# A state space mixer whose inputs are turned inside the gated embedding before it, and convolution taps queued behind each head's normalisation

## The chip, the cores and the metric

The kernel runs on one core of one Trainium2 chip. The metric is the device time of one execution in microseconds, as the median of several runs; less is better.

## What is computed

A token block of 512 rows by 1024 features passes two layers and then a second block. Each layer is a mixer, a convolutional feed-forward net and a gated embedding (`ple`), each with a residual. Layer 0's mixer is a gated MLP beside attention; layer 1's mixer is a complex state space model. The second block has two SwiGLU nets around a mixer of eight retention heads and a 31-tap depthwise convolution. The change touches these parts of the reference:

```python
def s5_mixer(u, ...):            # u = rms_norm(x, norm_mix[1])
    ...
    bu_re = jnp.einsum('gpc,bsgc->bsgp', bb_re, uf)
    bu_im = jnp.einsum('gpc,bsgc->bsgp', bb_im, uf)
    ...
    _, _, xr, xi = lax.associative_scan(_complex_affine_combine, (a_r, a_i, bu_re, bu_im), axis=1)
    y = (jnp.einsum('gcp,bsgp->bsgc', c_re.astype(f32), xr)
         - jnp.einsum('gcp,bsgp->bsgc', c_im.astype(f32), xi)
         + d.astype(f32).reshape(S5_GROUPS, S5_GROUP_CH) * uf)
...
        # end of each layer of the first block
        gate = jax.nn.sigmoid(rms_norm(x) @ ple_w_gate[i])
        x = x + gate * (p[i] @ ple_w_proj[i])
...
    # in the second block's mixer
    r = retention_chunkwise(q, k, v)
    r = ((r - mu) * lax.rsqrt(var + LN_EPS)).reshape(bsz, s, V_W) * ret_gn_g.astype(jnp.float32)
    ...
    u = lax.conv_general_dilated(u, conv_k, window_strides=(1,), padding=[(CONV_WIDTH - 1, 0)], ...)
```

## The kernel before

The activations lie in SBUF as eight tiles `x[0..7]` of 128 features by 512 tokens. A float32 product is made from three matmuls: both operands are split into a high and a low part (`Xh`, `Xl`, `whi`, `wlo`) and the low-by-low product is left out (L365 to L367). Weights come in the order of a list: `fetch` loads a raw tile by a DMA of SP's queue, `cook` (L339, L342) lets ACT cast the high part and DVE or POOL (GpSimd) subtract the low part, one tile ahead of the matmuls.

Each engine, and each queue of DMA issues (SP's and ACT's here), works strictly in order. Which order that is follows from the order in which the Python code is written and from a scheduler of the framework, which places instructions of one engine by its own estimates; tiles come from pools with a fixed number of buffers, and a write to a reused buffer waits for its last reader.

**The state space stage** stands between the gated embedding of layer 0 and the gated linear unit behind the mixer. Before it, the statistics of the RMS norm are summed (L204), spread over all partitions by a product of `diag` with ones (L197) and copied to `st_r` (L198). Then each of the eight groups k of 128 channels is a `Unit`:

- `drive` (L1226): DVE multiplies `x[k]` by gain and `st_r` into `h`, whose write to memory (`hd`, L1228) ACT's queue issues;
- `lift` (L1234): SP's queue reads it back in four pieces with time and channels turned, as `up`;
- `load` (L1221): SP's queue loads three tables, `tG`, `tE`, `tC`, two DMAs each;
- `mid`: 16 matmuls with `tG` (L1241, "feed" below), then six DVE operations with `tE` (L1244 to L1249, "spin" below), which rotate real and imaginary parts;
- `scan`: two scans on DVE (L1260), then six products and sums on POOL (L1267 to L1273; for odd k the real part's subtraction, L1269, on DVE), which give `xr` and `xi`;
- `emit`: 24 matmuls with `tC` (L1281), a GELU on ACT (L1283), and a way out through memory again (`y`, L1288);
- `land`: `y` is split into `Gh` and `Gl` for the matmuls of the linear unit ("G matmuls" below).

The loop over t runs `mid` of unit t, `scan` of t−1, `emit` of t−2, `land` of t−3 and the G matmuls of t−4. Of the two weight tiles that are held for the linear unit the first one's matmuls follow in the loop, the second one's after it.

**The heads.** Four rounds h2 of two heads each. `retain` takes the statistics of a head's 512x256 result from PSUM (L1606, L1607), copies the variances into `gnv` (L1610), forms the reciprocal root in `rstd_of` (L174 to L182, with a square root on ACT), and writes the normalised `rn` (L1613); `turn` has PE transpose `rn` (L1620). `taps(n)` issues n taps of the convolution (L1519), each one DVE operation that adds a shifted, scaled tile into PSUM.

Of the kernel before, what the change touches and what calls it, by code (L numbers as in the profile page):

```python
# [18 lines left out]
P = 128  # L19
# [30 lines left out]
def tile_net(ctx: ExitStack, tc: tile.TileContext, a, out):  # L50
# [273 lines left out]
    def cook(i):  # L324
        if i < len(plan):
# [16 lines left out]
            lo.tensor_tensor(lw, rv, hi.bitcast(F32), op=ALU.subtract)  # L342
# [857 lines left out]
    rms2 = Rms()  # L1200
    rb2 = ple(0, X, rms, rms2.add, (rms2.fin1, rms2.fin2))

    with tc.tile_pool(name="s5r", bufs=1) as rp:
# [5 lines left out]
        class Unit:  # L1209
# [4 lines left out]
            def load(self):  # L1214
                k = self.k
                self.G = rp.tile([P, 4, 256], F32, tag="tG", name=nm("tG"), bufs=2)
                self.E = rp.tile([P, 4, 256], F32, tag="tE", name=nm("tE"), bufs=2)
                self.C = rp.tile([P, 4, 448], F32, tag="tC", name=nm("tC"), bufs=2)
                for t, lo, hi in ((self.G, 0, 256), (self.E, 704, 960), (self.C, 256, 704)):
                    for i in range(2):  # L1220
                        nc.sync.dma_start(t[:, 2 * i:2 * i + 2, :],  # L1221
                                          tabs[2 * k + i].rearrange("p (q n) -> p q n", q=2)[:, :, lo:hi])

            def drive(self):
                h = rp.tile([P, 4, P], F32, tag="h", name=nm("h"), bufs=2)
                vec.scalar_tensor_tensor(h, x[self.k].rearrange("p (n j) -> p j n", j=4), col("norm_mix", KD + self.k),  # L1226
                                         rb2.rearrange("p (n j) -> p j n", j=4), op0=ALU.mult, op1=ALU.mult)
                nc.scalar.dma_start(hdr[self.k], h)  # L1228

            def lift(self):  # L1230
                self.up = rp.tile([P, 4, P], F32, tag=f"Gh{self.k}", name=nm("up"))
                src = hdr[self.k].rearrange("(i c) j n -> j c i n", c=32)
# [3 lines left out]
            def mid(self):  # L1236
                k, up = self.k, self.up
                self.pv = pv = [bank((P, 4, P)) for _ in range(2)]
                for z in range(2):
                    for i in range(4):  # L1240
                        pe.matmul(pv[z][:, i, :], self.G[:, i, P * z:P * z + P], up[:, i, :], start=True, stop=True)  # L1241
# [8 lines left out]
                self.rm = xt_(f"X{'hl'[self.par]}5")  # L1250
                act.copy(self.rm, r4[:, 4 * k:4 * k + 4].unsqueeze(2).to_broadcast([P, 4, P]))
                pool.memset(self.rm[:, :, 0:1], 0.0)

            def scan(self):
                k = self.k
                er, ei = self.E[:, :, 0:P], self.E[:, :, P:]
                zr = rp.tile([P, 4, P], F32, tag=f"Gl{k}", name=nm("zr"))
                zi = rp.tile([P, 4, P], F32, tag="zi", name=nm("zi"), bufs=2)
                for z, w in ((zr, self.pv[1]), (zi, self.pv[0])):
                    vec.tensor_tensor_scan(z.rearrange("p i n -> p (i n)"), self.rm.rearrange("p i n -> p (i n)"),  # L1260
                                           w.rearrange("p i n -> p (i n)"), 0.0, op0=ALU.mult, op1=ALU.add)
                self.xr = rp.tile([P, 4, P + 1], F32, tag="xr", name=nm("xr"), bufs=2)
# [3 lines left out]
                t = [xt_(f"X{'hl'[self.par]}{j}") for j in (2, 3)]  # L1266
                pool.tensor_tensor(t[0], er, zr, op=ALU.mult)  # L1267
                pool.tensor_tensor(t[1], ei, zi, op=ALU.mult)
                (vec if k % 2 else pool).tensor_tensor(self.xr[:, :, 1:], t[0], t[1], op=ALU.subtract)  # L1269
                v = [rp.tile([P, 4, P], F32, tag=f"v{j}", name=nm("v")) for j in range(2)]  # L1270
                pool.tensor_tensor(v[0], er, zi, op=ALU.mult)
                pool.tensor_tensor(v[1], ei, zr, op=ALU.mult)
                pool.tensor_tensor(self.xi[:, :, 1:], v[0], v[1], op=ALU.add)  # L1273

            def emit(self):
                k = self.k
                py = bank((P, 4, P))
                for i in range(4):
                    for st, (c, rhs) in enumerate(((320, self.up[:, i, :]), (32, self.xr[:, i, 0:P]),
                                                   (192, self.xi[:, i, 0:P]))):  # L1280
                        pe.matmul(py[:, i, :], self.C[:, i, c:c + P], rhs, start=st == 0, stop=st == 2)  # L1281
                g = rp.tile([P, 4, P], F32, tag="h", name=nm("g"), bufs=2)
# [7 lines left out]
            def land(self):  # L1290
                k = self.k
                G.h[k], G.l[k] = [rp.tile([P, T], F32R, tag=f"G{z}{k}", name=nm(f"G{z}")) for z in "hl"]
# [3 lines left out]
        units[0].load()  # L1296
        for u in units:
            u.drive()
        units[0].lift()
        units[1].load()  # L1300
        for u in units[1:]:
            u.lift()
        acc0, w0s = {}, {}
        for t in range(KD + 4):
            if t and t + 1 < KD:
                units[t + 1].load()
            if t < KD:
                units[t].mid()
            if 0 <= t - 1 < KD:
                units[t - 1].scan()  # L1310
# [4 lines left out]
            if 0 <= t - 3 < KD:  # L1315
                units[t - 3].land()
# [536 lines left out]
```

## Time and profile before

| what | us |
|---|---|
| median of 3 runs (2784.18 to 2787.91) | 2787.21 |
| the profiled execution's own time | 2786.97 |
| its span in the trace | 2785.2 |
| TensorE (PE) busy | 2698.1 |
| DVE busy | 1581.5 |
| ACT busy | 992.5 |
| POOL busy | 666.9 |

All durations below come from this one execution. PE is the engine with the most work; the others matter where PE waits for them. The row of the granted clock (PEclk) says at what share of its full speed PE ran in each of 40 slices.

### The profile page before, as it was taken

Reading aid. Unit: us, or ns where it says so; the run is one execution under the profiler, and the core shown is the slowest. Engines: PE = TensorE matmul, PEld = TensorE weight load, DVE = VectorE, ACT = ScalarE, POOL = GpSimd, SP = SyncE. Lnnn points to the kernel's source line nnn. Section 1 sums busy time; section 2 is a strip of 40 time slices with the busy share of each in tenths; the row PEclk is TensorE's granted clock in tenths of the full one; section 3 lists DMA queues with packets and bytes.
Section 4 is the critical chain, followed back from the end, with each engine's and each line's share of the span. In section 5 each row is a group of like instructions: output and inputs, shape, how many; then the busy total and the mean of one; then the engine's idle time right before and its main releaser. Section 6 shows DMA issues by size and latency. Waiting matters only on the chain. (4 is left out here: it accounts for less than half of the span.)

```text
span 2785.2 us, 35089 instructions
## 1 busy us (share of the span) xinstructions
PE 2698.1 (97%) x14355; PEld 2275.0 (82%) x14355; DVE 1581.5 (57%) x2478; ACT 992.5 (36%) x1295; POOL 666.9 (24%) x590
## 2 busy tenths in 40 slices
PE   8999999999579999999999999999999999999998
PEld 8978888887468888888888888887888788989888
DVE  5456968686654656466333335866387764733335
ACT  5544424344213423244212125333333352432222
POOL 2213035762351000002000026354443421300000
PEclk9999999999789999999999999999999999999999
DMA  5203334433762223224322232322222223222222
GB/s 162 76 31 107 99 105 148 148 132 133 224 207 91 91 91 101 96 76 136 101 96 91 92 105 82 95 82 81 97 81 97 76 91 109 89 91 91 91 95 72
DMA packets 277840, 289.80 MB, mean 104 GB/s; under 512 B 20197, under 2 KB 266951, under 8 KB 277680
## 3 DMA queue, kind: packets, MB, share of 16 engines
q1 hardware_dynamic: 256208, 260.38, 28.8%
q10 hardware_dynamic: 20640, 26.78, 2.7%
q8 instruction: 112, 1.84, 0.3%
q0 software_dynamic: 832, 0.41, 0.1%
q14 instruction: 48, 0.39, 0.0%
HBM read 263.43 MB, written 24.12 MB: 103 GB/s over the span
## 5 line engine op out<-in xcount | busy, mean ns | idle before, releaser
L339 ACT CAST whi<-raw 128x2048 fp32r<-128x2048 f32 (+2 forms) x216 | 406.3, 1881 | 761.4 <-PE ps L366 600.4
L365 PE MATMUL ps<-Xh,whi 128*128 128x512 f32 (+1 forms) x1472 | 567.4, 387 | 0.4 <-ACT Xh L302 0.4
L342 DVE TENSOR_TENSOR wlo<-raw,whi 128x2048 fp32r<-128x2048 f32 (+2 forms) x167 | 381.0, 2282 | 325.9 <-ACT whi L339 324.5
L366 PE MATMUL ps<-Xl,whi 128*128 128x512 f32 (+1 forms) x1472 | 563.0, 383 | 0.6 <-POOL Xl L305 0.6
L367 PE MATMUL ps<-Xh,wlo 128*128 128x512 f32 (+1 forms) x1472 | 562.7, 383 | 0.8 <-DVE wlo L342 0.8
L342 POOL TENSOR_TENSOR wlo<-raw,whi 128x2048 fp32r<-128x2048 f32 (+1 forms) x49 | 223.5, 4561 | 688.1 <-ACT whi L339 362.9
L365 PEld LDWEIGHTS ps<-Xh,whi 128*128 128x128 f32 x1472 | 276.2, 188 | 58.9 <-issue 3.2
L367 PEld LDWEIGHTS ps<-Xh,wlo 128*128 128x128 f32 x1472 | 276.7, 188 | 58.2 <-DVE wlo L342 1.6
L366 PEld LDWEIGHTS ps<-Xl,whi 128*128 128x128 f32 x1472 | 277.1, 188 | 56.9 <-issue 1.2
L365 PE MATMUL ps<-XBh,whi 128*128 128x512 f32 (+1 forms) x736 | 281.9, 385 | 1.0 <-ACT whi L339 1.0
L366 PE MATMUL ps<-XBl,whi 128*128 128x512 f32 (+1 forms) x736 | 281.0, 383 | 0.5 <-POOL XBl L305 0.5
L367 PE MATMUL ps<-XBh,wlo 128*128 128x512 f32 (+1 forms) x736 | 281.4, 384 | 0.0
L366 PE MATMUL ps<-Al,whi 128*128 128x512 f32 (+1 forms) x528 | 202.1, 383 | 1.5 <-DVE Al L305 1.5
L365 PE MATMUL ps<-Ah,whi 128*128 128x512 f32 (+1 forms) x528 | 202.6, 386 | 0.0
L367 PE MATMUL ps<-Ah,wlo 128*128 128x512 f32 (+1 forms) x528 | 202.5, 384 | 0.0
L1519 DVE SCALAR_TENSOR_TENSOR ps<-glu,par,ps 128x512 f32<-128x512 f32 x232 | 174.1, 751 | 4.1
L366 PEld LDWEIGHTS ps<-XBl,whi 128*128 128x128 f32 x736 | 138.2, 188 | 30.3 <-POOL XBl L305 0.9
L367 PEld LDWEIGHTS ps<-XBh,wlo 128*128 128x128 f32 x736 | 138.1, 188 | 29.9
L365 PEld LDWEIGHTS ps<-XBh,whi 128*128 128x128 f32 x736 | 137.6, 188 | 29.3 <-ACT whi L339 1.4
L222 POOL TENSOR_TENSOR st_a<-st_a,st_q 128x512 f32<-128x512 f32 x25 | 44.3, 1770 | 489.4 <-ACT st_q L220 489.3
L374 PE MATMUL ps<-whi,Xh 128*128 128x256 f32 (+1 forms) x512 | 147.6, 289 | 0.7 <-ACT z L608 0.4
L375 PE MATMUL ps<-wlo,Xh 128*128 128x256 f32 (+1 forms) x512 | 144.7, 283 | 0.0
(482 smaller groups left out, 4826.2 us busy)
## 6 DMA issues: line engine op xcount, KB each, us to landing
raw<-in_ffn_w_up_dram SPq DMA_DIRECT2D x66, 1024.0 KB, 5.1
raw<-in_w_in_dram SPq DMA_DIRECT2D x40, 1024.0 KB, 5.1
raw<-in_ffn_w_down_dram SPq DMA_DIRECT2D x32, 1024.0 KB, 4.8
raw<-in_ffn_w_gate_dram SPq DMA_DIRECT2D x22, 1024.0 KB, 5.2
tab<-tabs ACTq DMA_DIRECT2D x16, 960.0 KB, 3.9
raw<-in_ffn_w_down_dram SPq DMA_DIRECT2D x16, 768.0 KB, 4.1
raw<-in_ev_w_in_dram SPq DMA_DIRECT2D x8, 1024.0 KB, 5.2
raw<-in_ple_w_gate_dram SPq DMA_DIRECT2D x8, 1024.0 KB, 4.9
```

Of the source, the lines that this page charges most:

```text
L222: eng.tensor_tensor(self.acc, self.acc, sq, op=ALU.add)
L339: cp = act.copy(hi, rv)
L342: lo.tensor_tensor(lw, rv, hi.bitcast(F32), op=ALU.subtract)
L365: pe.matmul(acc, wh[j][:, s], X.h[k], start=start and t == 0, stop=False)
L366: pe.matmul(acc, wh[j][:, s], X.l[k], start=False, stop=False)
L367: pe.matmul(acc, wl[j][:, s], X.h[k], start=False, stop=stop and t == len(ks) - 1)
L374: pe.matmul(acc, X.h[k][:, s], wh[j], start=start and t == 0, stop=False)
L375: pe.matmul(acc, X.h[k][:, s], wl[j], start=False, stop=False)
L1519: vec.scalar_tensor_tensor(x[m] if t == 30 else acc, u[:, t:t + T], col("ck", t * KD + m), acc, op0=ALU.mult, op1=ALU.add)
```

## The change

Four edits.

1. In `cook`, a low part that POOL computes is subtracted in four quarters, four instructions in place of one.
2. The state space stage. ACT scales each `x[m]` by its gain alone (`turn_in`) as soon as the gated embedding has finished it, and the way through memory to `up` runs while the embedding goes on. After the statistics, `phases` makes one small tile `rbt` from the same product of ones and `diag`, and `norm` multiplies `up` by it: unit 0 on DVE, units 1 to 7 on POOL. Table loads move from SP's to ACT's queue, as separate calls (`load_g`, `load_e`, `load_c`), for units 0 and 1 (but for the latter's `tC`) and `tE` of unit 2 during the embedding; `tE` has three buffers in place of two. `mid` is cut into `feed`, now issued a turn earlier, and `spin`; the real part of an odd unit comes a turn later; unit 7's six products are all on DVE; part of the second weight tile's G matmuls move into the loop.
3. `retain` has no copy to `gnv`; it returns its last instruction.
4. The taps around `retain` are issued after that instruction: 8 (first head) or 24 (second head) taps behind the normalisation, none between statistics and `rn`.

```diff
-            lo.tensor_tensor(lw, rv, hi.bitcast(F32), op=ALU.subtract)
+            q = kt * n // 4 if lo is pool else kt * n
+            for o in range(0, kt * n, q):
+                lo.tensor_tensor(lw[:, o:o + q], rv[:, o:o + q], hi[:, o:o + q].bitcast(F32), op=ALU.subtract)
...
+            def table(self, tag, lo, hi, bufs):
+                t = ep.tile([P, 4, hi - lo], F32, tag=tag, name=nm(tag), bufs=bufs)
+                for i in range(2):
+                    nc.scalar.dma_start(t[:, 2 * i:2 * i + 2, :],
+                                        tabs[2 * self.k + i].rearrange("p (q n) -> p q n", q=2)[:, :, lo:hi])
+                return t
...
+            def turn_in(self):
                 k = self.k
+                h = ep.tile([P, 4, P], F32, tag="h", name=nm("h"), bufs=2)
+                act.activation(h, x[k].rearrange("p (n j) -> p j n", j=4), AF.Copy, scale=col("norm_mix", KD + k))
+                nc.scalar.dma_start(hdr[k], h)
+                self.up = ep.tile([P, 4, P], F32, tag=f"Gh{k}", name=nm("up"))
+                src = hdr[k].rearrange("(i c) j n -> j c i n", c=32)
                 for b in range(4):
                     nc.sync.dma_start(self.up[32 * b:32 * b + 32], src[3 - b])
...
+            def norm(self, eng):
+                eng.tensor_tensor(self.up, self.up, rbt.unsqueeze(1).to_broadcast([P, 4, P]), op=ALU.mult)
...
+                eng = vec if k == KD - 1 else pool
...
+        def ready(m):
+            rms2.add(m)
+            units[m].turn_in()
+            if m == 1:
+                units[0].load_g()
+                units[0].load_e()
+            elif m == 3:
+                units[1].load_g()
+                units[1].load_e()
+            elif m == 5:
+                units[0].load_c()
+                units[2].load_e()
+
+        def phases():
+            b = bank((P, P, 4))
+            pe.matmul(b.rearrange("p n j -> p (n j)"), ones, rms2.dg.rearrange("p i t -> p (i t)"),
+                      start=True, stop=True)
+            for j in range(4):
+                r = slice(32 * j, 32 * j + 32)
+                (vec.tensor_copy if j % 2 else act.copy)(rbt[r], b[r, :, 3 - j])
...
+        ple(0, X, rms, ready, (rms2.fin1, phases))
...
         for t in range(KD + 4):
...
+            if at(t + 1):
+                at(t + 1).feed()
+            if at(t + 3):
+                at(t + 3).load_g()
+            if at(t):
+                at(t).spin()
+                if at(t - 1) and t % 2 == 0:
+                    at(t - 1).real(vec)
...
-                vv = sm.tile([P, NT], F32, tag="gn_v", name=nm("gnv"))
-                vec.tensor_copy(vv, mv[:, :, 1])
-                r = rstd_of(vv, NT, LN_EPS)
+                r = rstd_of(mv[:, :, 1], NT, LN_EPS)
...
-                hd_.retain()
-                taps(8)
-            taps(16)
+                with tc.issue_after(hd_.retain().ins):
+                    taps(8 if j == 0 else 24)
```

**First place: DVE where the state space units begin.** Before the change, the last three of the eight products `h` stand ahead of unit 0's six operations (with `tE` and the PSUM banks `ps`) and its two scans.

```order
L1226 SCALAR_TENSOR_TENSOR h_6582<-x_77,par,st_r_6550 128x512
L1226 SCALAR_TENSOR_TENSOR h_6585<-x_78,par,st_r_6550 128x512
L1226 SCALAR_TENSOR_TENSOR h_6588<-x_79,par,st_r_6550 128x512
L1244 TENSOR_TENSOR s_889_6650<-tE_6559,ps_6640 128x512
L1245 TENSOR_TENSOR ps_6640<-tE_6559,ps_6640 128x512
L1246 TENSOR_TENSOR s_890_6651<-tE_6559,ps_6641 128x512
L1247 TENSOR_TENSOR ps_6641<-tE_6559,ps_6641 128x512
L1249 TENSOR_TENSOR ps_6640<-s_890_6651,ps_6640 128x512
L1248 TENSOR_TENSOR ps_6641<-s_889_6650,ps_6641 128x512
L1260 SCALAR_TENSOR_TENSOR zi_6692<-s_891_6658,ps_6640 128x512
L1260 SCALAR_TENSOR_TENSOR zr_6691<-s_891_6658,ps_6641 128x512
L1244 TENSOR_TENSOR s_897_6680<-tE_6597,ps_6670 128x512
```

With the change, the row of `diag` is followed at once by the two copies to `rbt`, by `norm` of unit 0 and by its operations; the scans are L1269.

```order
L190 TENSOR_TENSOR diag_880_6638<-cst_80,rr_879_6633 128x512
L1334 COPY rbt_6052<-ps_885_6660 32x128 x2
L1241 TENSOR_TENSOR up_816_6299<-up_816_6299,rbt_6052 128x512
L1257 TENSOR_TENSOR s5_894_6707<-tE_822_6323,ps_886_6671 128x512
L1258 TENSOR_TENSOR ps_886_6671<-tE_822_6323,ps_886_6671 128x512
L1259 TENSOR_TENSOR s5_895_6708<-tE_822_6323,ps_887_6672 128x512
L1260 TENSOR_TENSOR ps_887_6672<-tE_822_6323,ps_887_6672 128x512
L1262 TENSOR_TENSOR ps_886_6671<-s5_895_6708,ps_886_6671 128x512
L1261 TENSOR_TENSOR ps_887_6672<-s5_894_6707,ps_887_6672 128x512
L1269 SCALAR_TENSOR_TENSOR zi_897_6716<-s5_888_6681,ps_886_6671 128x512
L1269 SCALAR_TENSOR_TENSOR zr_896_6715<-s5_888_6681,ps_887_6672 128x512
L1257 TENSOR_TENSOR s5_908_6750<-tE_832_6361,ps_890_6691 128x512
```

The eight products are gone from this place, and one product of the same size stands there. The next unit follows directly.

**Second place: the table loads.** Before, SP's queue: the rows of unit 0's three tables, unit 1's `tG`, unit 0's `up`, and unit 1's `tE` and `tC` begin.

```order
L1221 DMA tG_6558<-tab_2507 128x2x256
L1221 DMA tG_6558<-tab_2508 128x2x256
L1221 DMA tE_6559<-tab_2507 128x2x256
L1221 DMA tE_6559<-tab_2508 128x2x256
L1221 DMA tC_6560<-tab_2507 128x2x448
L1221 DMA tC_6560<-tab_2508 128x2x448
L1221 DMA tG_6596<-tab_2509 128x2x256
L1221 DMA tG_6596<-tab_2510 128x2x256
L1234 DMA up_6591<-hd_2523 32x4x128 x4
L1221 DMA tE_6597<-tab_2509 128x2x256
L1221 DMA tE_6597<-tab_2510 128x2x256
L1221 DMA tC_6598<-tab_2509 128x2x448
```

With the change, ACT's queue right behind the copies to `rbt`: DMA issues for `tG` of units 2 to 5 and `tE` of unit 3 stand in one order with a cast of weights (`whi`) and with the copies `s5` that the scans of units 1 and 2 need.

```order
L1217 DMA tG_889_6684<-tab4_2535 128x2x256
L1217 DMA tG_889_6684<-tab5_2536 128x2x256
L1217 DMA tG_893_6704<-tab6_2537 128x2x256
L1217 DMA tG_893_6704<-tab7_2538 128x2x256
L1217 DMA tG_907_6747<-tab8_2539 128x2x256
L1250 COPY s5_906_6744<-r4_2530 128x512
L1217 DMA tG_907_6747<-tab9_2540 128x2x256
L1217 DMA tG_922_6792<-tab10_2541 128x2x256
L1217 DMA tG_922_6792<-tab11_2542 128x2x256
L339 CAST whi_926_6806<-raw_863_6560 128x2048
L1250 COPY s5_921_6789<-r4_2530 128x512
L1217 DMA tE_930_6812<-tab6_2537 128x2x256
```

The loads have moved to an engine that computes between them.

**Third place: DVE in the last head.** Before, from the copy `gnv` on, taps (L1519, `ps<-glu`) stand between the short operations of `rstd_of`; the next row is the first of `rn`.

```order
L1610 COPY gnv_16720<-mv_16675 128x4
L1519 SCALAR_TENSOR_TENSOR ps_16666<-glu_16150,par,ps_16666 128x512
L174 TENSOR_SCALAR rv_16722<-gnv_16720 128x4
L1519 SCALAR_TENSOR_TENSOR ps_16666<-glu_16150,par,ps_16666 128x512 x3
L179 RECIPROCAL rr_16726<-rt_16724 128x4
L1519 SCALAR_TENSOR_TENSOR ps_16666<-glu_16150,par,ps_16666 128x512
L180 SCALAR_TENSOR_TENSOR rt_16724<-rv_16722,rr_16726 128x4
L1519 SCALAR_TENSOR_TENSOR ps_16666<-glu_16150,par,ps_16666 128x512
L181 TENSOR_TENSOR rt_16724<-rt_16724,rr_16726 128x4
L1519 SCALAR_TENSOR_TENSOR ps_16666<-glu_16150,par,ps_16666 128x512
L182 SCALAR_TENSOR_TENSOR rr_16726<-rt_16724,rr_16726 128x4
L1519 SCALAR_TENSOR_TENSOR ps_16666<-glu_16150,par,ps_16666 128x512
```

With the change, from the last statistics to the first tap:

```order
L1671 BN_AGGR mv_2272_16814<-bs_2277_16853 128x2
L1671 BN_AGGR mv_2272_16814<-bs_2278_16856 128x2
L174 TENSOR_SCALAR rv_2279_16859<-mv_2272_16814 128x4
L179 RECIPROCAL rr_2281_16863<-rt_2280_16861 128x4
L180 SCALAR_TENSOR_TENSOR rt_2280_16861<-rv_2279_16859,rr_2281_16863 128x4
L181 TENSOR_TENSOR rt_2280_16861<-rt_2280_16861,rr_2281_16863 128x4
L182 SCALAR_TENSOR_TENSOR rr_2281_16863<-rt_2280_16861,rr_2281_16863 128x4
L1675 TENSOR_SCALAR rn_2271_16813<-ps_2273_16815,mv_2272_16814,rr_2281_16863 128x256 x2
L1675 TENSOR_SCALAR rn_2271_16813<-ps_2276_16831,mv_2272_16814,rr_2281_16863 128x256 x2
L1583 SCALAR_TENSOR_TENSOR ps_2270_16805<-glu_2201_16279,par_117,ps_2270_16805 128x512 x4
```

The taps have gone behind `rn`, and the copy is gone.

## Rows read from the trace of the kernel before

**Rows 1.** The page: busy time, share, instructions; granted clock in 40 slices (tenths).

```profile
PE 2698.1 (97%) x14355; PEld 2275.0 (82%) x14355; DVE 1581.5 (57%) x2478; ACT 992.5 (36%) x1295; POOL 666.9 (24%) x590
...
PEclk9999999999789999999999999999999999999999
```

**Rows 2.** Windows: PE, PEld, DVE, ACT, POOL busy (x instructions), PE clock, DMA share, GB/s.

```profile
640.00:714.65 74.65, 73.33 (x329) 58.70 (x328) 43.72 (x59) 40.20 (x57) 11.14 (x12) 1.00 0.43 140
...
714.65:736.99 22.34, 3.76 (x17) 3.49 (x16) 8.80 (x8) 0.58 (x1) 0.00 (x0) 0.61 0.94 303
736.99:825.06 88.07, 56.99 (x339) 51.21 (x340) 63.30 (x79) 16.14 (x24) 60.38 (x62) 0.75 0.69 210
825.06:839.30 14.24, 14.24 (x63) 11.13 (x63) 2.26 (x4) 5.54 (x8) 0.00 (x0) 1.00 0.38 111
```

**Rows 3.** What PE waited for: us in total, times, longest us.

```profile
PE ps L1241 <- DMA up<-hd: 19.5, 2, 13.4
PE ps L1241 <- DMA tG<-tab: 12.7, 3, 10.9
PE ps L365 <- ACT Gh L302: 10.6, 3, 6.0
PE ps L1620 <- DVE rn L1613: 8.4, 4, 3.4
```

**Rows 4.** Timeline at the stage's start: start, duration, engine, instruction, idle before.

```profile
713.57 1.08 PE L197 MATMUL ps<-diag,ones 128*128 128x512 f32 x2
...
714.76 0.58 ACT L198 COPY st_r<-ps 128x512 f32<-128x512 f32 x1 [0.40 <-PE ps L197]
...
716.53 20.91 ACTq L1228 DMA_DIRECT2D hd<-h  x8
...
728.08 3.75 PE L1241 MATMUL ps<-up,tG 128*128 128x128 f32 x16 [13.42 <-DMA up<-hd]
...
736.99 0.68 DVE L1244 TENSOR_TENSOR s<-tE,ps 128x512 f32<-128x512 f32 x1
...
740.58 1.21 DVE L1260 TENSOR_TENSOR_SCAN zi<-s,ps 128x512 f32<-128x512 f32 x1
741.71 1.19 DVE L1260 TENSOR_TENSOR_SCAN zr<-s,ps 128x512 f32<-128x512 f32 x1
741.87 1.26 POOL L1268 TENSOR_TENSOR s<-tE,zi 128x512 f32<-128x512 f32 x1 [27.82 <-DVE zi L1260]
```

**Rows 5.** Line L1221, the table loads: from issue to landing.

```profile
DMA to landing us min/median/max: 3.0/5.4/11.2
```

**Rows 6.** DVE's other operations, 737 to 825: busy, mean ns, idle before.

```profile
L1269 DVE TENSOR_TENSOR xr<-s,s 128x512 f32<-128x512 f32 x4 | 6.2, 1560 | 8.5 <-POOL s L1267 8.5
...
L305 DVE TENSOR_TENSOR Gl<-y,Gh 128x512 fp32r<-128x512 f32 x5 | 4.5, 901 | 5.2 <-ACT Gh L302 5.2
...
L342 DVE TENSOR_TENSOR wlo<-raw,whi 128x2048 fp32r<-128x2048 f32 x1 | 2.3, 2307 | 1.4 <-ACT whi L339 1.4
```

**Rows 7.** Timeline of PE at the end of the stage: unit 7's last emit passes.

```profile
822.65 0.49 PE L1281 MATMUL ps<-xi,tC 128*128 128x128 f32 x2 [0.63 <-POOL xi L1273]
```

**Rows 8.** Timeline of POOL, DVE, ACT and PE in the last head.

```profile
2159.70 4.61 POOL L342 TENSOR_TENSOR wlo<-raw,whi 128x2048 fp32r<-128x2048 f32 x1 [6.64 <-ACT whi L339]
...
2161.61 2.72 DVE L1610 COPY gnv<-mv 128x4 f32<-128x4 f32 x1
...
2165.09 0.21 ACT L177 ACTIVATE rt<-rv 128x4 f32<-128x4 f32 x1 [4.17 <-DVE rv L174]
...
2170.44 1.89 DVE L1613 TENSOR_SCALAR rn<-ps,mv,rr 128x256 f32<-128x256 f32 x4
...
2171.12 0.66 PE L1620 MATMUL ps<-cst,rn 128*128 128x128 f32 x2 [3.35 <-DVE rn L1613]
```

**Rows 9.** Windows behind that wait, columns as in rows 2.

```profile
2170.00:2175.00 5.00, 3.88 (x17) 3.61 (x18) 2.99 (x6) 0.00 (x0) 0.00 (x0) 0.54 0.00 0
2175.00:2180.00 5.00, 5.00 (x20) 3.96 (x20) 3.99 (x6) 1.24 (x2) 2.59 (x2) 0.78 0.00 2
```

More of the change, by code (lines that the diff above doesn't have):

```diff
@@ L1233, in lift, with feed @@
                 for b in range(4):
                     nc.sync.dma_start(self.up[32 * b:32 * b + 32], src[3 - b])
-            def mid(self):
-                k, up = self.k, self.up
-                self.pv = pv = [bank((P, 4, P)) for _ in range(2)]
+            def norm(self, eng):
+                eng.tensor_tensor(self.up, self.up, rbt.unsqueeze(1).to_broadcast([P, 4, P]), op=ALU.mult)
+            def feed(self):
+                self.pv = [bank((P, 4, P)) for _ in range(2)]
                 for z in range(2):
@@ L1291, in land, with at @@
                 k = self.k
-                G.h[k], G.l[k] = [rp.tile([P, T], F32R, tag=f"G{z}{k}", name=nm(f"G{z}")) for z in "hl"]
+                G.h[k] = ep.tile([P, T], F32R, tag=f"Gh{k}", name=nm("Gh"))
+                G.l[k] = rp.tile([P, T], F32R, tag=f"Gl{k}", name=nm("Gl"))
                 split(G.h[k], G.l[k], self.y.rearrange("p r n -> p (r n)"))
         units = [Unit(k) for k in range(KD)]
[L1296 to L1302, printed above, removed]
+        def ready(m):
[13 more added lines that the diff above has]
+            pe.matmul(b.rearrange("p n j -> p (n j)"), ones, rms2.dg.rearrange("p i t -> p (i t)"),
+                      start=True, stop=True)
+            for j in range(4):
+                r = slice(32 * j, 32 * j + 32)
+                (vec.tensor_copy if j % 2 else act.copy)(rbt[r], b[r, :, 3 - j])
+        rbt = ep.tile([P, P], F32, name="rbt")
+        ple(0, X, rms, ready, (rms2.fin1, phases))
+        rp = late.enter_context(tc.tile_pool(name="s5r", bufs=1))
+        def at(k):
+            return units[k] if 0 <= k < KD else None
+        units[0].norm(vec)
+        units[0].feed()
+        units[2].load_g()
+        for k in range(1, 5):
+            units[k].norm(pool)
         acc0, w0s = {}, {}
         for t in range(KD + 4):
[L1305 to L1310, printed above, removed]
+            if at(t + 1):
[6 more added lines that the diff above has]
+                    at(t - 1).real(vec)
             if t == 2:
@@ L1314, in tile_net @@
                 acc0[1] = [bank() for _ in range(2)]
-            if 0 <= t - 3 < KD:
-                units[t - 3].land()
-            if 0 <= t - 2 < KD:
-                units[t - 2].emit()
-            if 0 <= t - 4 < KD:
-                k = t - 4
-                mm_fm(acc0[1], w0s[1], G, [k], start=k == 0, stop=k == KD - 1, js=[k])
+            if t > 1 and at(t + 1):
+                at(t + 1).load_e()
+            if t == KD:
+                acc0[0] = [bank() for _ in range(2)]
+                mm_fm(acc0[1], w0s[1], G, [4], start=False, stop=False, js=[4])
+                for k in range(3):
+                    mm_fm(acc0[0], w0s[0], G, [k], start=k == 0, stop=False, js=[k])
+            if at(t - 2):
+                at(t - 2).emit()
+            if t and at(t):
+                at(t).load_c()
+            if at(t):
+                at(t).scan()
+                if at(t + 5):
+                    at(t + 5).norm(pool)
+            if at(t - 3):
+                at(t - 3).land()
+            if at(t - 4):
+                k = t - 4
+                if t != KD:
+                    mm_fm(acc0[1], w0s[1], G, [k], start=k == 0, stop=k == KD - 1, js=[k])
+                if t == KD + 1:
+                    for j in (3, 4, 5):
+                        mm_fm(acc0[0], w0s[0], G, [j], start=False, stop=False, js=[j])
+                elif t > KD + 1:
+                    mm_fm(acc0[0], w0s[0], G, [k], start=False, stop=k == KD - 1, js=[k])
             if t == KD:
@@ L1327, in tile_net @@
                 fetch(nxt[0] + 1)
-        acc0[0] = [bank() for _ in range(2)]
-        mm_fm(acc0[0], w0s[0], G, K8)
         X = new_x()
```

77 lines of the change are left out of this document (37 added, 40 removed).

## The prediction

> **What bounds the kernel now.** The page comes first: TensorE (PE) is busy for 2698.1 of 2785.2 us, DVE for 57%, ACT for 36%, POOL for 24% [rows 1]. So PE is the bound nearly everywhere, and there is little to gain but its idle 87.1 us and the time that it runs at a low clock. The row of the granted clock shows one dip, in the eleventh and twelfth slice, which is 696 to 836 us [rows 1].
>
> The list of PE's waits says which work ends last there. The four longest of those that the change touches are the inputs `up` of the state space units (19.5 us), their tables `tG` (12.7), their outputs `Gh` (10.6), and, elsewhere, the normalised heads `rn` (8.4) [rows 3]. That is 51 of the 87 us.
>
> The windows show the state space stage in three parts. Up to 714.65 the gated embedding keeps PE full at full clock. Then PE works for 3.76 of 22.34 us at a clock of 0.61: it waits for the inputs to be scaled, written out and read back. From 736.99, when DVE starts on unit 0, to 825.06, when the last unit's `emit` ends, PE works for 56.99 of 88.07 us at 0.75. After that it is full again [rows 2]. The second part gives 88.07 / 8 = 11.0 us for a unit. Neither DVE (63.30 us, 7.9 a unit) nor POOL (60.38, 7.5 a unit) fills it; the waits for `tG` and `Gh` lie here. The reader is to see that the stage is a chain of latencies: what ends it is the last unit, and PE has little to do meanwhile.
>
> **The change part by part.** All sums are made against the profiled execution, 2786.97 us, which is 0.24 below the median.
>
> *Start of the stage.* Before, from the end of the product with ones (714.65) to the first spin operation (736.99), 22.34 us go into `st_r`, eight products `h`, the write to memory and the read back, in which SP's queue has the loads of eight table halves ahead of the first `up`. PE waits 13.42 us for that one `up` [rows 2, 4]. With the change all this lies in the embedding. What is left after the product with ones:
> - the statistics come later, because the ACT queue now issues the write of the eighth `h` and table loads ahead of the square root. No row shows this wait; it costs between 0 and one landing, of 5.4 us median [rows 5]. I take 2, nearer to nothing, since only what is issued ahead of the last `h` can stand there.
> - two copies one behind the other, on ACT and on DVE, to `rbt`, at no more than the 0.58 of the full copy to `st_r`: 1.2 [rows 4].
> - `norm` of unit 0, a product of two SBUF tiles, as L1269: 1.6 [rows 6].
> - half of the first feed, one bank, at the low clock: 3.75 / 2 = 1.9 [rows 4].
>
> The first spin then starts at 714.65 + 2 + 1.2 + 1.6 + 1.9 = 721.4, or 15.6 earlier.
>
> *The units.* With tables two and three units ahead, DVE is what is left as the chain. Six operations take 740.58 − 736.99 = 3.59 us and a scan 1.13, so a unit takes 5.85, and eight take 46.8 [rows 4]. To these come three real parts of 1.56 (4.7), one low part of weights (2.3), some five `Gl` of 0.90 before the end (4.5) [rows 6], and unit 7's six products, now on DVE, at the price of `Gl` (5.4): 63.7 in all, to 785.1. From the last `xi` to the end of the last emit PE needs 825.06 − 822.65 = 2.4 [rows 2, 7]: 787.5. Waits for tables do not vanish: I leave a third of the 12.7 us of `tG` [rows 3], 4.2, between nothing and the whole of the present 11.0 a unit (rival 1). The end of the last emit moves from 825.06 to 791.7, which is worth 33.4.
>
> POOL's chain stays beside this: seven `norm` and then units 0 to 6 with five or six operations of 1.26 each [rows 4], 7 × 1.26 + (4 × 6 + 3 × 5) × 1.26 = 58 us from about 719, to 777. So it has 8 us to spare. The transfers do too: the second window moved 210 GB/s × 88.07 = 18.5 MB, and the first ran at 303 GB/s with the DMA engines 0.94 busy [rows 2]; at that rate 18.5 MB take 61 us, from 717 to 778. That is close, and is why I leave a wait.
>
> *Linear unit.* In the new order 48 G matmuls stand on PE ahead of the end of the last emit, and 34 in the old. The 14 more fall into idle time and are missing from the full stretch behind, where one takes 14.24 / 63 = 0.226 us [rows 2]: 3.2.
>
> *What the embedding pays.* Eight more ACT operations at about 0.58 make 4.6 us [rows 4]; ACT is busy for 40.20 of 74.65 us there, DVE for 43.72 [rows 2], and so PE hides it. Nothing. If the ACT queue's DMA issues held up its sigmoids and weight casts, PE would pay up to those 4.6 us.
>
> *Quarters in `cook`.* The subtraction of 4.61 us [rows 8] becomes four of about 1.15 to 1.26 [rows 4]: at most 0.4 us more on an engine that is idle for three quarters of the time, and no wait of PE on POOL's low part is among those listed. Nothing for itself.
>
> *Heads.* In the last head the copy `gnv` takes 2.72 us from 2161.61, and it ends at 2164.33 just as POOL's subtraction ends, at 2164.31. Then taps stand between the short operations, `rn` starts at 2170.44, and PE has waited 3.35 us by 2171.12 [rows 8]. Without the copy and the taps 8.83 us shrink to four short operations and the square root of 0.21 [rows 8]; I estimate 1.5. If each of the four had to wait for one POOL quarter of 4.61 / 4 = 1.15, it would be 6.1, `rn` would start at 2167.7, and of the 3.35 us 0.6 would stay. So the heads' 8.4 us [rows 3] go, or at least 5.4, twice the long wait's 2.7. Behind the last wait PE ran at 0.54 for 3.88 busy us and at 0.78 for 5.00 [rows 9]: 0.46 × 3.88 + 0.22 × 5.00 = 2.9 us lost to the clock. Whether the wait or the sparse work behind it lowered the clock these rows do not say; I take half, 1.4. Sum 9.8, with bounds of 5.4 and 11.3. The displaced taps are late by as much as `rn` is early, and the last one ends where it did.
>
> *Sum.* 33.4 + 3.2 + 9.8 = 46.4. 2786.97 − 46.4 = 2740.6, and with the 0.24 to the median **2741**.
>
> **A rule against it.** The copy that ends with POOL's operation shows DVE held up for as long as an operation of POOL lasts [rows 8], and L1269 costs 1.56 on average against 0.90 for `Gl` [rows 6]. The Trainium skill, "SBUF — State Buffer", section "Who interferes with whom", says that a DVE instruction with two SBUF inputs and a GpSimd instruction that reads SBUF exclude each other for the whole instruction. The trace agrees with it for the copy, and less clearly for `Gl`. Here it speaks against the change, which packs DVE and POOL closer: by the rows' means the sum is 2741, by a full exclusion it is that of rival 2.
>
> **Rivals.**
> 1. *Only the start pays.* The tables go on coming at the old pace, since the same bytes pass the same engines, and a unit still takes 11.0. For it: 0.94 of DMA share in the first window, landings of up to 11.2 us [rows 2, 5]. Against it: 3 tables of the first units are loaded during the embedding, with the DMA engines 0.43 busy [rows 2]. The last emit ends at 721.4 + 88.1 = 809.5; gain 15.6 + 3.2 + 9.8 = 28.6: **2759**, or 2763 with the heads at 5.4.
> 2. *DVE and POOL block each other.* Three real parts, five `Gl` and the low part each wait for a whole POOL operation of 1.26 [rows 4]: 11.3, of which 3 × (1.56 − 0.90) = 2.0 are already in the mean of L1269 that I used [rows 6]. The end comes 9.3 later: **2750**. For it: the copy [rows 8]. Against it: `Gl` at 0.90 beside a busy POOL [rows 6].
> 3. *The heads stay as they are*, as `rn` is held up by POOL's quarters, or by another operation that comes last: **2751**. Against it: the bound of 5.4 above.
> 4. *Slower: the ACT queue blocks itself.* The table loads now stand in one order with the copies for the scans, the GELUs and the `Gh` casts. Were each of a unit's three tables to hold the queue for one landing of 5.4 us [rows 5], a unit would take 16.2, the last emit would end at 721.4 + 129.6 = 851.0, and 25.9 − 3.2 − 9.8 = 12.9 would be lost: **2800**. It turns against the change from (825.06 + 3.2 + 9.8 − 721.4) / 8 = 14.6 us a unit. For it: eight writes take 20.91 us on that queue now, each one behind a landing [rows 4]. Against it: two or three buffers of each table let the loads overlap.
> 5. *Nothing is in the way:* the statistics are not late, no table is waited for, the heads give all. 33.4 + 2 + 4.2 + 3.2 + 11.3 = 54.1: **2733**.
>
> **How the numbers follow.** The forecast, 2741 give or take 6, has 0.50; rival 1 0.17, rival 2 0.12, rival 3 0.08, rival 5 0.05, rival 4 0.05; 0.03 is for rivals 1 and 4 in part, which end near no change. The range takes in rival 5 and rival 1 with the heads' lower bound: 2730 to 2764; outside it lie rival 4 and the case near no change, and some of the edges. Within 0.2%, or 5.6 us, is about what a measurement of this kernel can't tell from no change. Faster 0.92, same 0.03, slower 0.05.
>
> **What would show it.** Right: PE's wait for `up` nearly gone; the first spin operation 7 us or so behind the product with ones; DVE nearly without gaps from there, and a unit every 8 us; the dense G matmuls from 792 on a clock counted from the same product; no wait of PE for `rn`, or four below 1 us. Wrong: waits for `tG` or `tE` that grow; a scan that waits for the copy `s5` of ACT (rival 4); L1269 and `Gl` above 2 us (rival 2); PE's waits in the embedding, which would move the whole stage. The steps that I trust least are the 4.2 us of table waits and the 2 us of late statistics.

## The result, and the profile after

The changed kernel takes 2757.93 us (median of 4 runs, 2756.88 to 2759.23) against 2786.05 before; the ratio is 0.9899, with a 95% interval of 0.9882 to 0.9916. It is 28 us faster. The forecast was 2741 in a range of 2730 to 2764: sign and range hold, but of the 46 us that the sum gave only 28 came, and the "2741 give or take 6" that had a chance of 0.50 was missed by 17.

The page of the changed kernel has the busy times and the granted clock in one place; the columns are those of [rows 1].

```profile
PE 2701.6 (98%) x14355; PEld 2274.9 (83%) x14355; DVE 1564.2 (57%) x2470; ACT 1001.6 (36%) x1304; POOL 691.3 (25%) x739
...
PEclk9999999999999999999999999999999999999999
```

The dip of the clock is gone from the row of slices (the windows below still show a mean of 0.87 for the units). The span fell by 29.7 us, to 2755.5, but the busy time of PE rose by 3.5 us with the same 14355 matmuls, although the clock is higher. That is the first sign of something that was in no step of the prediction.

The list of PE's waits of the changed kernel answers to [rows 3]:

```profile
PE ps L1298 <- POOL xr L1290: 8.2, 2, 4.7
PE ps L1247 <- DVE zr L1269: 5.0, 2, 4.7
...
PE ps L1298 <- DVE xr L1290: 3.0, 2, 2.5
...
PE ps L1247 <- DMA tG<-tab: 1.1, 1, 1.1
```

The waits for `up` (19.5), for `Gh` (10.6) and for `rn` (8.4) are not in it any more, and `tG` fell from 12.7 to 1.1. New are waits for POOL's `xr` (8.2) and for the scans' `zr` (5.0), and that for DVE's `xr` grew from 1.4 to 3.0: within the stage the chain of computation ends last now, not the transfers.

The windows of the changed kernel, cut at the same events as [rows 2] (end of the product with ones, first spin operation, end of the last emit):

```profile
640.00:716.71 76.71, 74.06 (x332) 59.30 (x330) 42.04 (x59) 47.61 (x64) 11.11 (x12) 1.00 0.76 250
716.71:719.93 3.22, 1.16 (x11) 1.19 (x11) 1.27 (x3) 0.51 (x2) 1.91 (x2) 1.00 0.27 104
719.93:799.65 79.72, 58.40 (x361) 52.69 (x360) 64.31 (x81) 15.49 (x23) 58.96 (x63) 0.87 0.65 193
799.65:813.60 13.95, 13.95 (x61) 11.31 (x61) 3.62 (x6) 4.20 (x7) 0.00 (x0) 1.00 0.49 132
```

The stretch from the statistics to the first spin shrank from 22.34 to 3.22 us; the units took 79.72 us, or 10.0 each, against 11.0. The last emit ends at 799.65 and not at 791.7.

To see where along the kernel time is gained and lost, one compares the starts of the same instruction in both traces. ACT casts one weight tile after another, 220 in all (216 at L339, four at L302):

| cast | before | changed | shift |
|---|---|---|---|
| 58, in the gated embedding | 700.78 | 700.42 | −0.4 |
| 64, behind the stage | 883.84 | 855.37 | −28.5 |
| 128 | 1584.69 | 1559.85 | −24.8 |
| 140, ahead of the heads | 1742.29 | 1718.49 | −23.8 |
| 180, behind the heads | 2263.23 | 2229.74 | −33.5 |
| 220, the last | 2742.51 | 2712.56 | −30.0 |

So the stage gave 28.1 us, the heads 9.7, and in the dense stretches between and behind them, whose matmuls the change doesn't touch, 8.2 were lost again.

### The profile page after: what moved, and what is told of

Read it like the earlier page. It is cut to its first block, busy times and chain, and to the rows that moved or that the text cites. A ratio compares the mean times of both kernels' runs of the same rounds, so it can differ in the third digit from the quotient of the medians.

```text
span 2755.5 us, 35269 instructions
## 1 busy us (share of the span) xinstructions
PE 2701.6 (98%) x14355; PEld 2274.9 (83%) x14355; DVE 1564.2 (57%) x2470; ACT 1001.6 (36%) x1304; POOL 691.3 (25%) x739
## 5 line engine op out<-in xcount | busy, mean ns | idle before, releaser
L339 ACT CAST whi<-raw 128x2048 fp32r<-128x2048 f32 (+2 forms) x216 | 406.4, 1881 | 765.4 <-PE ps L368 597.0
L344 POOL TENSOR_TENSOR wlo<-raw,whi 128x512 fp32r<-128x512 f32 (+1 forms) x196 | 248.4, 1300 | 669.8 <-ACT whi L339 342.0
```

The lines of the kernel that those rows point to most:

```text
L339: cp = act.copy(hi, rv)
L344: lo.tensor_tensor(lw[:, o:o + q], rv[:, o:o + q], hi[:, o:o + q].bitcast(F32), op=ALU.subtract)
```

## The experiments

Twelve kernels ran, in three groups of four. Each was timed beside the kernel before, whose median was 2786.42, 2787.30 and 2787.95 in the three groups. Numbers in brackets behind a median are its ratio to that and the 95% interval of the ratio. The median of the kernel before differs by up to 1.5 us from group to group, so a difference of that size between kernels of two groups says nothing.

### Where the 8 us of the dense stretches went

In the changed kernel every pool behind the pool of small tiles lies 96 bytes lower, as the compiled program's memory map shows: the tile `gnv`, which had three buffers of 32 bytes there, is gone. Three kernels put a dead tile in its place, of one, two or three such buffers (`bufs` 1, 2 and 3 for `pad32`, `pad64` and `pad96`). But for this memset on POOL, all engines have the same instructions, and in the traces they run in the same order (on ACT a DMA issue changes places with a neighbour here and there).

```diff
     vec.memset(eps_l, LN_EPS)
+    pool.memset(sm.tile([P, 8], F32, tag="pad", name="pad", bufs=3), 0.0)
```

`pad96`:

> The changed kernel with one dead tile of three buffers of 32 bytes put where the pool of small tiles lost the tile gnv; the instructions of every engine stand in the same order. Theory 'address': every pool behind it lies 96 bytes lower since gnv is gone, and that alone slows the dense matmuls there from 231.1 to 233.3 ns a step; so the step in the net between 1300 and 1650 us goes back to 231.1 ns, and the time falls by the slip of about 8 us, to 2750. Rival 'pace of the run': the step comes from the new schedule or from the run, and the time stays at 2758.

`pad64`:

> As the run before, with 64 bytes of padding. Theory 'address', in the form that the start of the moving tile counts by its remainder to 64 bytes: this padding changes nothing, the step stays at 233.3 ns and the time at 2758. If any move away from the new address helped, it would be about 2750. Rival 'pace of the run': 2758 here too, so this run only tells together with the other two.

`pad32`:

> As the two runs before, with 32 bytes of padding. Theory 'address' by the remainder to 64 bytes: the step falls to 231.1 ns or below, the time to 2750 or a little less. If only the old address is good: 2758. Rival 'pace of the run': 2758.

Measured: 2751.32 (ratio 0.988, 0.9863 to 0.9896), 2760.33 (0.9907, 0.9893 to 0.9922) and 2747.51 (0.9865, 0.9851 to 0.988). The window from 1300 to 1600 us lies in a feed-forward net that the change leaves alone. PE is full and the granted clock 1.00 in all five kernels; what differs is how many matmuls (in brackets) start in 300 us. First the kernel before, then one by one the changed kernel, `pad96`, `pad64` and `pad32`:

```profile
1300.00:1600.00 300.00, 300.00 (x1301) 244.11 (x1300) 111.28 (x99) 79.16 (x78) 12.80 (x8) 1.00 0.29 95
```

```profile
1300.00:1600.00 300.00, 300.00 (x1287) 241.47 (x1286) 96.15 (x79) 71.98 (x66) 0.42 (x1) 1.00 0.28 93
```

```profile
1300.00:1600.00 300.00, 300.00 (x1300) 243.83 (x1299) 96.09 (x79) 71.94 (x66) 0.00 (x0) 1.00 0.29 94
```

```profile
1300.00:1600.00 300.00, 300.00 (x1286) 241.17 (x1285) 96.12 (x79) 72.22 (x67) 2.27 (x2) 1.00 0.28 93
```

```profile
1300.00:1600.00 300.00, 300.00 (x1308) 245.61 (x1307) 96.66 (x80) 73.16 (x68) 2.55 (x2) 1.00 0.30 97
```

64 bytes leave the pace of the changed kernel, 96 bring back that of before, and 32 a better one. "Pace of the run" falls; "address", by the remainder to 64 bytes, holds in all three. The casts of the table above say the same of the whole kernel: in the two dense stretches (casts 64 to 140 and 180 to 220) the changed kernel lost 8.2 us against the kernel before, `pad64` 9.6 and `pad96` 0.8, while `pad32` gained 1.6. That 32 bytes are better still than 96 was not priced. The pace shows it, and the 2.4 us of the dense stretches; the 3.8 us between the two medians do not by themselves, since the intervals overlap. The last section has the table.

### What held the units up: a memset of four columns

```diff
-                self.xr = rp.tile([P, 4, P + 1], F32, tag="xr", name=nm("xr"), bufs=2)
-                self.xi = rp.tile([P, 4, P + 1], F32, tag="xi", name=nm("xi"), bufs=2)
-                pool.memset(self.xr[:, :, 0:1], 0.0)
-                pool.memset(self.xi[:, :, 0:1], 0.0)
+                self.xr, self.xi = XR[k % 2], XI[k % 2]
...
+        XR, XI = [[rp.tile([P, 4, P + 1], F32, tag=f"{z}{i}", name=nm(z)) for i in range(2)] for z in ("xr", "xi")]
+        for b in XR + XI:
+            pool.memset(b[:, :, 0:1], 0.0)
```

The timeline of POOL in the changed kernel, from the end of unit 0 to unit 1's products:

```profile
733.26 1.29 POOL L1287 TENSOR_TENSOR xi<-s,s 128x512 f32<-128x512 f32 x1
734.46 0.13 POOL L1251 MEMSET s<- 128x4 f32 x1
738.93 0.10 POOL L1275 MEMSET xr<- 128x4 f32 x1 [4.34 <-PE ps L1298]
739.36 0.11 POOL L1276 MEMSET xi<- 128x4 f32 x1 [0.32 <-PE ps L1298]
739.42 1.26 POOL L1279 TENSOR_TENSOR s<-tE,zi 128x512 f32<-128x512 f32 x1
```

and of DVE, in the same kernel:

```profile
743.16 1.73 DVE L1290 TENSOR_TENSOR xr<-s,s 128x512 f32<-128x512 f32 x1 [7.79 <-POOL s L1278]
...
757.92 0.69 DVE L1257 TENSOR_TENSOR s<-tE,ps 128x512 f32<-128x512 f32 x1 [1.70 <-DMA tE<-tab]
...
765.40 1.73 DVE L1290 TENSOR_TENSOR xr<-s,s 128x512 f32<-128x512 f32 x1 [3.20 <-POOL s L1278]
```

The memsets at 738.93 belong to unit 2, which reuses unit 0's buffers, and so they wait until unit 0's emit has read them. They need 0.1 us each, but unit 1's products stand behind them in POOL's order, and DVE's real part of unit 1, with the scans of unit 2 behind it, waits for those. DVE is idle for 7.79 and 3.20 us that way, 11.0 in all.

`once`:

> The changed kernel with the two buffers each of xr and xi allocated once and their first column cleared once ahead of the units, so that no memset stands on POOL between the units. Theory 'memset': on POOL the memset for unit k+1 stands ahead of the products of unit k and waits for the emit of unit k-1 to have read that buffer (11.8 us in all), and DVE then waits for POOL (11.0 us); without it the last emit ends about 8 us earlier and the time is 2750. Rival 'emit chain': the waits only move on to the tables, to ACT's copies or to the next product; less than 2 us, 2756 to 2758.

Measured: 2749.82 (0.9874, 0.9859 to 0.9888), 8.1 below the changed kernel, and 10.5 below `pad64`, which has the same slow pace and ran in the same group. In the trace of `once` the same two stretches read, POOL first and then DVE:

```profile
732.34 1.26 POOL L1284 TENSOR_TENSOR xi<-s,s 128x512 f32<-128x512 f32 x1
733.55 0.10 POOL L1251 MEMSET s<- 128x4 f32 x1
733.61 1.26 POOL L1276 TENSOR_TENSOR s<-tE,zi 128x512 f32<-128x512 f32 x1
```

```profile
737.35 1.75 DVE L1287 TENSOR_TENSOR xr<-s,s 128x512 f32<-128x512 f32 x1 [3.03 <-POOL s L1275]
...
753.93 0.69 DVE L1257 TENSOR_TENSOR s<-tE,ps 128x512 f32<-128x512 f32 x1 [3.50 <-DMA tE<-tab]
```

POOL goes on at once, the wait of 7.79 is 3.03, the other one is gone. Part of it turned into a wait for a table, 3.50 in place of 1.70. The 3.03 that stay are POOL's own work: it has seven `norm` and the six products of unit 0 ahead of those of unit 1. The last emit ends at 793.50, which is 6.2 earlier; the first spin was 0.9 earlier, so the units gained 5.3. That is more than chance: from the first spin to the end of the last emit the units take 79.7 to 80.5 us in the changed kernel and its three padded forms, and 74.5 in `once`. "Memset" holds; of the 8 us that it asked for in the stage 2 are missing, in part because the wait moved on to a table, as "emit chain" has it. The time fell by 7.1 us between the two profiled executions.

### The heads: three edits, one wait

`heads_only` is the kernel before with the diff's last two pieces and a padding of 96 bytes. `s5_only` is the changed kernel with both of these edits undone:

```diff
-                r = rstd_of(mv[:, :, 1], NT, LN_EPS)
+                vv = sm.tile([P, NT], F32, tag="gn_v", name=nm("gnv"))
+                vec.tensor_copy(vv, mv[:, :, 1])
+                r = rstd_of(vv, NT, LN_EPS)
...
-                with tc.issue_after(hd_.retain().ins):
-                    taps(8 if j == 0 else 24)
+                hd_.retain()
+                taps(8)
+            taps(16)
```

`copy_kept` has the first of the two alone, `taps_kept` the second alone and 96 bytes of padding.

`heads_only`:

> The kernel before with the two edits of the heads alone (no copy to gnv, taps behind the normalisation), and with 96 bytes of padding, so that no later tile moves. By the prediction's term the four waits of PE for rn (8.4 us) and a part of the low clock go: 9.8 us, 2776. By rival 3 another operation comes last and the time stays within 2 us of before, 2784 to 2786.

`s5_only`:

> The changed kernel with the heads' two edits undone; gnv is there, so later tiles lie where they lay before. The shift of the stage read from the changed kernel's trace was 28.4 us, so 2758; PE's waits for rn are back at about 8 us and the dense step is 231.1 ns. If the state space part had given the predicted 36.6, it would be 2750; if only its start paid (rival 1, 18.8), 2767.

`taps_kept`:

> The changed kernel with 96 bytes of padding, the copy to gnv left out, but the taps issued around the normalisation as before. Theory 'taps': the taps between the short operations delay rn; most of the 8.4 us of waits is back, 2756 to 2759 against 2751 of the padded change. Theory 'copy': the copy's wait for POOL was what delayed rn, and leaving it out is enough: 2751 to 2753.

`copy_kept`:

> The changed kernel with the copy to gnv back (so no padding is needed) and the taps behind the normalisation. Theory 'taps': nothing waits for the copy, 2751 to 2752. Theory 'copy': the copy again lasts as long as POOL's operation; as POOL's subtraction now comes in quarters of 1.2 us, it could cost up to that in each head, 1 to 5 us, 2752 to 2756.

Measured: 2776.79 (0.9963, 0.995 to 0.9975), 2752.12 (0.9876, 0.9863 to 0.9889), 2748.75 (0.9866, 0.9852 to 0.9879) and 2749.82 (0.9868, 0.9853 to 0.988). The heads' edits alone give 10.5 us, as forecast. The forecast for `s5_only`, 2758 with waits for `rn` of about 8 us, was missed: the changed kernel without them is as fast as `pad96` with them, to within 1 us, and undoing one of the two loses nothing. So neither "taps" nor "copy" can be the only cause: something else in the change already did the same. What is left in `s5_only` is the quarters of `cook`. The group of DVE's copies in its trace, which lasted 2159 ns in the median before:

```profile
L174 DVE TENSOR_SCALAR rv<-gnv 128x4 f32<-128x4 f32 x8 | 6.2, 776 | 0.0
L1674 DVE COPY gnv<-mv 128x4 f32<-128x4 f32 x8 | 5.8, 720 | 0.0
```

and PE's wait for `rn` in the same trace, which was 8.4 before:

```profile
PE ps L1685 <- DVE rn L1677: 3.5, 2, 1.8
```

The copies last 0.72 us. The operation behind them (L174), which took 0.155 us before, now takes 0.78 beside the next quarter, so that the two together went from 2.3 to 1.5. The third group tested the quarters:

```diff
-            lo.tensor_tensor(lw, rv, hi.bitcast(F32), op=ALU.subtract)
+            q = kt * n // 4 if lo is pool else kt * n
+            for o in range(0, kt * n, q):
+                lo.tensor_tensor(lw[:, o:o + q], rv[:, o:o + q], hi[:, o:o + q].bitcast(F32), op=ALU.subtract)
```

`quarters_only` is this in the kernel before; `no_quarters` undoes it in `pad96`.

`quarters_only`:

> The kernel before with the one edit of the quarters: POOL's low parts in four instructions. The prediction gave this edit nothing, 2786. Theory 'short lock', after the run with the heads' edits undone: with POOL's operation of 1.2 us in place of 4.6 the copy gnv lasts 0.7 in place of 2.2 us, and that alone takes most of PE's waits for rn; 7 to 8 us, 2779.

`no_quarters`:

> The changed kernel with 96 bytes of padding and with POOL's low parts in one instruction again. Theory 'short lock': the heads' edits alone gave 8.8 us in the trace, with the quarters 10.3; so 1 to 2 us come back, 2752 to 2753, unless a whole operation of 4.6 us meets one of the short operations of the reciprocal root. Rival 'the quarters carry the heads': 6 to 8 us come back, 2758.

Measured: 2777.17 (0.9959, 0.9944 to 0.9975) and 2753.66 (0.9875, 0.9856 to 0.9893). The quarters alone give 10.8 us, or 7 to 16 by the interval; "short lock" holds. PE's wait for `rn` in `quarters_only`:

```profile
PE ps L1622 <- DVE rn L1615: 3.5, 2, 1.8
```

It is 3.5 in place of 8.4 us. Undone in the changed kernel they cost 2.3, which the intervals don't tell from nothing. There the first short operation has taken over what the copy did: in `no_quarters` the eight that read the variances last 2.8 us on average. In the last head it ends just as POOL's whole operation ends (2136.36 and 2136.33):

```profile
L175 DVE TENSOR_SCALAR rv<-mv 128x4 f32<-128x4 f32 x8 | 22.2, 2773 | 0.1
```

```profile
2131.72 4.61 POOL L343 TENSOR_TENSOR wlo<-raw,whi 128x2048 fp32r<-128x2048 f32 x1 [6.66 <-ACT whi L340]
...
2132.46 3.90 DVE L175 TENSOR_SCALAR rv<-mv 128x4 f32<-128x4 f32 x1
```

PE has no wait for `rn` in that trace, in which no taps stand between the operations that follow.

The casts free this from the pace of the dense stretches. From cast 140 to cast 180, which takes in all the heads, the gain against the kernel before is

| in the kernel | quarters | no copy | taps behind | us |
|---|---|---|---|---|
| `quarters_only` | yes | | | 8.3 |
| `s5_only` | yes | | | 7.7 |
| `heads_only` | | yes | yes | 8.8 |
| `no_quarters` | | yes | yes | 7.2 |
| `copy_kept` | yes | | yes | 10.4 |
| `taps_kept` | yes | yes | | 11.1 |
| `pad96` | yes | yes | yes | 10.3 |

Either the quarters or the two other edits take 7 to 9 us, and all three together 10: they shorten the same wait. With the quarters, one of the two others is as good as both. Which of the two counts without the quarters was not run.

### Both causes mended, and the tables' queue

`once_pad32` joins two edits above. `tables_sp` is that with all table loads on SP's queue:

```diff
-                    nc.scalar.dma_start(t[:, 2 * i:2 * i + 2, :],
+                    nc.sync.dma_start(t[:, 2 * i:2 * i + 2, :],
```

`once_pad32`:

> The changed kernel with the columns of xr and xi cleared once and with 32 bytes of padding. If the two causes are independent, their gains add: 2757.9 less 8.1 less 10.4, or 2739. If the stage's waits differ with the placement, 2741 to 2745.

`tables_sp`:

> As the run before (columns cleared once, 32 bytes of padding), but every table load on SP's queue again. Rival 4 in part: if the loads on ACT's queue hold up ACT's copies and one another, the DVE waits for tE (4.5 us in the run with the columns cleared once) shrink and the time falls by 2 to 4 us. Other way: on SP's queue the loads stand ahead of the reads of up and y, which come later; the time rises by 2 to 15 us, and PE waits for up or for Gh.

Measured: 2740.04 (0.9826, 0.9807 to 0.9844) and 2742.15 (0.9833, 0.9815 to 0.9852). The two gains add, to within 1 us. This is the best version: 48 us faster than the kernel before in its group, 18 faster than the changed kernel. On SP's queue DVE's waits for `tE` are gone, but the last emit ends at 796.56 and not at 794.57, since the first spin was 0.6 later and a wait of 3.6 us for POOL took their place; the 2 us between the two times are within their intervals. Which queue loads the tables doesn't matter to what these runs can tell.

## Why the prediction was right, and by how much it was off

- **The range** held by luck. It was made to reach to rival 1, whose mechanism is not what happened; the forecast itself came out 17 us too low, half of it in the stage and half in a place where the sum had nothing.
- **The start of the stage** was right to 1.5 us. The statistics came 2.06 later (716.71 against 714.65), as much as assumed, but only half of it for the reason given. ACT's last two products `h` stand ahead of the last square of the statistics, and each takes 1.2 us, where the sum had priced such an operation at 0.58:

```profile
707.26 2.31 ACT L1233 ACTIVATE h<-x,par 128x512 f32<-128x512 f32 x2
...
709.46 0.64 ACT L220 ACTIVATE st_q<-x 128x512 f32<-128x512 f32 x1
...
709.97 0.95 ACTq L915 DMA_DIRECT2D pjd<-Xh  x2
...
710.96 1.07 ACT L910 COPY Xl<-ps 128x512 f32<-128x512 f32 x2 [0.86 <-ACT st_q L220]
```

  The last square started at 708.40 before, so 1.06 us come from there. The other 1.0 is nearer to the reason given: ACT's copies `Xl`, which stand ahead of the root, wait 0.86 us behind the square while the queue issues two writes `pjd`. The first spin started at 719.93; the sum had 721.4. The copies took 1.27, as priced (1.2); `norm` took 0.69 and not 1.6, and the half feed 1.27 and not 1.9, at a granted clock of 1.00.
- **The units.** The step that failed is "POOL's chain stays beside this", which left the waits for tables, 4.2 us, as the only wait. DVE was busy for 64.31 us, where the sum had 63.7. The waits for tables were 1.70. What was missing is the 11.0 us of waits for POOL: the last emit ended 8.0 later than forecast (11.0 more for POOL and 1.1 more from the last `xi` to the end of the last emit, less 2.5 for tables and 1.5 at the start). DVE's busy time came out as summed only in total: the low part took 3.35 and not 2.3, five `Gl` 5.6 and not 4.5, unit 7's products 4.1 and not 5.4. Clearing the columns once takes 8.0 of the 11.0 away. The "8 us to spare" added up POOL's busy time and left out what POOL itself waits for. That waiting instruction could be read in the old trace, in the groups of POOL's instructions in the window 737 to 825 of the kernel before (count, busy, mean ns, idle time ahead and what ended it):

```profile
L1264 POOL MEMSET xr<- 128x4 f32 x6 | 0.6, 103 | 7.7 <-PE ps L1281 7.7
```

The prediction passed over it, since the instruction itself is so short.
- **The G matmuls** were right: beyond the 25.4 us by which the last emit moved, cast 64 moved by 28.5 − 25.4 = 3.1 us more, against 3.2.
- **The embedding** paid 2.65 us of idle PE time ahead of the end of the product with ones, where 1.32 stood before, for "nothing". ACT's eight products took 9.7 us there, not 4.6.
- **The heads** were right in sum, 9.7 in the trace against 9.8, though the quarters, which the sum left out, take much of the same wait. All of the low clock went, not half: behind the last `rn`, which starts at 2136.20, the granted clock is 1.00, where it was 0.54 and 0.78.

```profile
2136.00:2141.00 5.00, 5.00 (x31) 4.32 (x31) 4.86 (x9) 0.00 (x0) 0.15 (x1) 1.00 0.64 210
2141.00:2146.00 5.00, 4.37 (x18) 3.04 (x18) 4.03 (x7) 1.24 (x2) 2.58 (x2) 1.00 0.00 0
```

  Right too was the bound that each short operation may wait for a quarter; in the last head of the changed kernel two of them last 1.22 us beside POOL's quarters, where 0.15 to 0.17 is usual:

```profile
2133.70 1.22 DVE L181 TENSOR_TENSOR rt<-rt,rr 128x4 f32<-128x4 f32 x1
2134.95 1.22 DVE L182 SCALAR_TENSOR_TENSOR rr<-rt,rr 128x4 f32<-128x4 f32 x1
```

- **"Quarters: nothing for itself"** was wrong as a reason, though not in the sum. They were priced by what PE waits for on POOL, and what they shorten is how long POOL holds up DVE. Alone they take as much as the two edits of the heads.
- **No step at all** had the 8.2 us that the dense matmuls lost. It is the second half of the error: 8.0 in the stage, 8.2 here. That removing a tile of a few bytes moves every later one was visible in the code; its price was not visible in any row.
- **The rivals.** Rival 1, "only the start pays", is near in its time, 2759, but for another reason: the tables came in time. Rival 2, the mutual blocking of DVE and POOL, is real for the small operations (above) and for the real parts at 1.73, and for `Gl` at up to 1.64, but cost the stage little beyond the sum, whose prices were means of rows beside a busy POOL. The copies shrink from 2.2 to 0.7 us when POOL's operation shrinks from 4.6 to 1.3; a copy has one SBUF input, so it is not the case of two inputs that the prediction took it for. The operations with two are L181 and L182, at 1.22 beside the quarters. The Trainium skill, "SBUF — State Buffer", "Who interferes with whom", names copies and `tensor_scalar` too among those that can take the ports shared with GpSimd, and the trace agrees with both cases. Rival 4, the ACT queue blocking itself, costs nothing that these runs can tell: in `tables_sp` the waits for `tE` are gone, and it is no faster.

## What to carry to other kernels

Before a chain is called "beside the path", list not only what its engine does but what each instruction on it waits for, the smallest ones too: a memset of 0.1 us that waits for a buffer holds up everything behind it. If three edits shorten one wait, test them one by one, since their gains need not add, as here. And when a stretch that a change doesn't touch gets slower at the same granted clock, compare where the tiles lie in memory, before and after.

## What the runs showed of the hardware

The pace of full matmuls (128x512, f32, weights 128x128) depends in these runs on where the moving tile starts in SBUF. The traces show it without any address. The tiles `Xh` and `Xl` lie ahead of the padding, and their matmuls take 230.0 to 230.2 ns from one start to the next in the kernel before, the changed kernel and the three padded ones alike. `XBh` and `XBl` lie behind it; theirs take 231.1 before, 233.3 in the changed kernel, and 233.7, 231.1 and 229.7 with 64, 96 and 32 bytes of padding.

The addresses are in the memory map alone, not in the traces. For six kernels the matmuls of the split products were taken in order from the trace and from the compiled program's memory map, with the time from one start to the next (those of 215 to 245 ns), and averaged by the remainder of the moving tile's start to 128 bytes. The weights' start has remainder 96 in nearly all of them.

| remainder | mean ns, lowest and highest of the kernels | matmuls before | matmuls changed | in `pad32` |
|---|---|---|---|---|
| 0 | 233.4 to 233.7 | none | 95 | 505 |
| 32 | 231.2 to 231.7 | 4026 | none | 94 |
| 64 | 233.2 to 233.4 | 505 | 4037 | none |
| 96 | 229.9 to 230.1 | 4034 | 4440 | 7970 |

The matmuls that went from remainder 32 to 64, some 4030, lost 233.27 − 231.25 = 2.02 ns each: 8.1 us. The 505 that went from 64 to 96 gained some 3.3 ns each, or 1.7, so 6.5 are left; `pad96` took 6.6 off the changed kernel's time. In the dense stretches 8.2 were lost, so a part of these is not explained by the table. `pad32` puts nearly all at 96. Whether the remainder itself counts, or its distance from that of the weights, these runs don't tell, since the weights were never moved; nor do they show what in the chip makes the difference.
